# Half-height rotary score matmuls, run as pairs in the two row halves of TensorE

## The chip, the cores and the metric

The kernel runs on one core of a Trainium2 chip. The metric is device time in microseconds (us) of one execution; several executions are timed and their median is taken. Beside them stands one execution recorded by the hardware profiler, with every instruction of the engines: TensorE (PE, with its weight loads as PEld), VectorE (DVE), ScalarE (ACT), GpSimd (POOL) and the queue engine SyncE (SP).

## What is computed

One encoder layer for two sequences of 1024 tokens and width 1024, in float32. A projection feeds two branches, latent attention with four heads and Fourier mixing; both go through one output projection, then a gated feed-forward part. The change concerns the attention scores only:

```
sc = (einsum('bqhd,bkhd->bhqk', q_nope, k_nope)
      + einsum('bqhr,bkr->bhqk', q_pe, k_pe)) * scale
p = softmax(sc, axis=-1)
o = einsum('bhqk,bkhd->bqhd', p, v)
```

The first product goes over 128 latent values per head, the second over the 64 rotary values (ROPE_DIM = 64) of the query `q_pe` and of the key `k_pe`, which all heads share.

## The kernel before

To keep float32 precision with the fast matmul type, each operand is split into a high and a low part, and a product is made of high*high, high*low and low*high (`mm3`, lines 78 to 80; `split`, lines 62 and 63, is an ACT cast followed by a DVE subtraction).

The program runs in stages: input projection and Fourier input, Fourier output, attention with the output projection, then feed-forward for both sequences. The attention stage handles 64 items in the order sequence s (2), query block b (4 of 256 rows), head h (4), query tile u (2 of 128 rows). Item k = 8*(4*s + b) + 2*h + u. I call the eight items of one query block a batch.

For item k the main loop issues, in this order: `scores(k)`; parts of the preparation of the next batch's queries (`rope_q`, `rope_flip`); after an odd item `absorb_q` of the next head (L78 to L80, `gb<-wq,ql`, followed by the split into `qa`); `flip_p(k-1)`, which turns the probabilities of the item before by eight TensorE transposes (L929, `ppt<-ident,p`); after a whole head `values` (L78 to L80, `gb<-pt,ckv`, 24 matmuls); and a step of the output projection and second norm of an older batch (`out_step`: 12 matmuls `gb<-wv,o`, then L813, and per row tile `norm2` with the square sum L821 on ACT, the reciprocal root on POOL L102 to L109 and the scaling L823 `xn` on DVE, then the transposes L833). A scheduler may shift the order inside each engine; each engine then runs its own list strictly in order.

`scores` of an item makes a tile `ps_s` of 128 queries x 1024 keys in PSUM, of which there are two buffers. Each half of 512 keys is summed by five matmuls, L903 to L907: three for the latent part (`qa`), two for the rotary part (`qp`). The rotary operands use all 128 rows of the array: rows 0 to 63 of `qp` hold the high part of q_pe, rows 64 to 127 the low part, and both row halves of `lat[i][:, 1]` hold the same 64 rows of k_pe, in its high part for i = 0 and its low part for i = 1. So L906 gives (high + low)*high, and L907 (high + low)*low. Then the softmax follows: the maximum on DVE (L912 `mx`), its scaled negative (L913 `nb`), the exponential with the row sum on ACT (L915, two records: ACTIVATE and the reading of the accumulator), the reciprocal (L916 `rr`) and the scaling (L917 `p`) on DVE. The exponential is the last reader of the `ps_s` tile; a tile's buffer is free for other scores only behind it.

Of the kernel before, what the change touches and what calls it, by code (L numbers as in the profile page):

```python
# [12 lines left out]
F32 = mybir.dt.float32  # L13
# [3 lines left out]
ALU = mybir.AluOpType  # L17
# [4 lines left out]
P = 128  # L22
D = 1024
N = 1024
# [28 lines left out]
def hybrid_encoder_kernel(ctx: ExitStack, tc: tile.TileContext, a: dict):  # L53
    nc = tc.nc
# [3 lines left out]
    def rd(t):  # L58
        return t.bitcast(F32)
# [17 lines left out]
    def mm3(out, lh, ll, rh, rl, first, last, cont=False):  # L77
        nc.tensor.matmul(out, lh, rh, start=first, stop=False, skip_group_check=cont)  # L78
        nc.tensor.matmul(out, lh, rl, start=False, stop=False, skip_group_check=cont)  # L79
        nc.tensor.matmul(out, ll, rh, start=False, stop=last, skip_group_check=cont)  # L80
# [82 lines left out]
    with ExitStack() as st:  # L163
# [3 lines left out]
        pp = st.enter_context(tc.tile_pool(name="p1_ps", bufs=8, space=PSUM, reuse_waits="tile"))  # L167
# [394 lines left out]
    S = {}  # L562
# [11 lines left out]
    def half(name):  # L574
        return e.tile([P, 512], F32, tag="hv", name=name, bufs=2)
# [34 lines left out]
    with ExitStack() as st:  # L610
# [3 lines left out]
        pp = st.enter_context(tc.tile_pool(name="p2_ps", bufs=8, space=PSUM, reuse_waits="tile"))  # L614
# [179 lines left out]
    def gbank():  # L794
        return tl_ps.tile([P, 512], F32, tag="g", name="gb", bufs=2)
# [55 lines left out]
    with ExitStack() as st:  # L851
        w = st.enter_context(tc.tile_pool(name="p3", bufs=1, side="right", reuse_waits="tile"))
        pp = st.enter_context(tc.tile_pool(name="p3_ps", bufs=1, space=PSUM, reuse_waits="tile"))
        st.enter_context(E3)

        def rope_q(s, b, u):
            ql = S["q", s, b]
            ti = 2 * b + u
            us = slice(u * P, u * P + P)
            pq = gbank()  # L860
            for c in range(2):
                mm3(pq[:, :256], ql[0][:, c, us], ql[1][:, c, us], wq_h[:, c, 512:], wq_l[:, c, 512:], c == 0, c == 1)
            pv = pq[:, :256].rearrange("p (h r) -> p h r", h=HEADS)
            t1 = half("qt1").rearrange("p (k h r) -> p k h r", k=2, h=HEADS)
            cb = rc[:, ti : ti + 1, :].broadcast_to([P, HEADS, ROPE])
            sb = rs[:, ti : ti + 1, :].broadcast_to([P, HEADS, ROPE])
            nc.vector.tensor_tensor(out=t1[:, 0], in0=pv, in1=cb, op=ALU.mult)
            nc.vector.tensor_tensor(out=t1[:, 1, :, :32], in0=pv[:, :, 32:], in1=sb[:, :, :32], op=ALU.mult)
            nc.vector.tensor_tensor(out=t1[:, 1, :, 32:], in0=pv[:, :, :32], in1=sb[:, :, 32:], op=ALU.mult)
            here["p"] = nc.gpsimd.tensor_tensor(out=t1[:, 0], in0=t1[:, 0], in1=t1[:, 1], op=ALU.add).ins  # L870
            sk = w.tile([P, HEADS, P], F32R, tag="sk", name="qsk", bufs=2)
            nc.scalar.copy(sk[:, :, :64], t1[:, 0])
            nc.vector.tensor_tensor(out=sk[:, :, 64:], in0=t1[:, 0], in1=rd(sk[:, :, :64]), op=ALU.subtract)
            S["sk", s, b, u] = sk

        def rope_flip(s, b, u):
# [8 lines left out]
        def absorb_q(s, b, h):  # L885
# [6 lines left out]
            split(qa[0], qa[1], pq[:, :256])  # L892
            S["qa", s, b, h] = qa

        def scores(s, b, h, u):
            lat = S[s][0]
            qa, qp = S["qa", s, b, h], S["qp", s, b, u]
            us = slice(u * P, u * P + P)
            ps = pp.tile([P, N], F32, tag="s", name="ps_s", bufs=2)
            for g in range(2):  # L900
                gs = slice(512 * g, 512 * g + 512)
                o = ps[:, gs]
                nc.tensor.matmul(o, qa[0][:, us], lat[0][:, 0, gs], start=True, stop=False)  # L903
                nc.tensor.matmul(o, qa[0][:, us], lat[1][:, 0, gs], start=False, stop=False)
                nc.tensor.matmul(o, qa[1][:, us], lat[0][:, 0, gs], start=False, stop=False)
                nc.tensor.matmul(o, qp[:, h, :], lat[0][:, 1, gs], start=False, stop=False)  # L906
                nc.tensor.matmul(o, qp[:, h, :], lat[1][:, 1, gs], start=False, stop=True)  # L907
            mx = tiny.tile([P, 1], F32, name="mx")
            nb = tiny.tile([P, 1], F32, name="nb")
            sm = tiny.tile([P, 1], F32, name="sm")  # L910
            rr = tiny.tile([P, 1], F32, name="rr")
            nc.vector.tensor_reduce(out=mx, in_=ps, axis=AX.X, op=ALU.max)  # L912
            nc.vector.tensor_scalar(out=nb, in0=mx, scalar1=-SCALE, scalar2=None, op0=ALU.mult)  # L913
            p = w.tile([P, N], F32, tag="p", name="p", bufs=3)
            nc.scalar.activation(p, ps, AF.Exp, bias=nb, scale=SCALE, accum_out=sm)  # L915
            nc.vector.reciprocal(rr, sm)  # L916
            nc.vector.tensor_scalar(out=p, in0=p, scalar1=rr[:, 0:1], scalar2=None, op0=ALU.mult)  # L917
            S["p", s, b, h, u] = p
            S["rr"] = rr
# [23 lines left out]
        for u in range(2):  # L943
            rope_q(0, 0, u)
# [52 lines left out]
        for k in range(nit + 4):  # L997
# [7 lines left out]
            if k < nit:  # L1005
                s, b, h, u = items[k]
                scores(s, b, h, u)
                nxt = items[k + 8 - k % 8] if k + 8 - k % 8 < nit else None
                i = k % 8
                if nxt is not None:  # L1010
                    if i == 0:
                        load_q(*nxt[:2])
                    if i == 3 and nxt[1] == 0:
                        load_seq(nxt[0], w)
                    if i in (3, 4):
                        rope_q(*nxt[:2], i - 3)
                    if i in (5, 6):
                        rope_flip(*nxt[:2], i - 5)
                if u == 1 and k + 1 < nit:
                    absorb_q(*items[k + 1][:3])  # L1020
# [14 lines left out]
    with ExitStack() as st:  # L1035
# [139 lines left out]
        pp = st.enter_context(tc.tile_pool(name="p5_ps", bufs=8, space=PSUM, reuse_waits="tile"))  # L1175
# [455 lines left out]
```

## Time and profile before

| what | value |
|---|---|
| median of the 3 timed runs | 2117.27 us (2114.76 to 2119.18) |
| span of the profiled execution, first to last instruction | 2109.8 us |
| PE busy in it | 2033.0 us (96%), 10044 matmuls |
| DVE / ACT / POOL busy | 67% / 43% / 39% |
| attention stage, first to last score matmul | about 335 to 764 us |
| PE busy in 335 to 764 us | 412.72 of 429 us |
| mean granted TensorE clock of the core | 0.988 |

The page gives no other time for the profiled execution than its span; the timed runs lie some 7.5 us above it, which is what lies around the first and the last instruction. A matmul record lasts longer than its slot, since matmuls overlap in the array: a record of 128x512 lasts 0.39 us, but the next one starts 0.23 us later. So what a matmul costs is read from the distance of the starts.

### The profile page before, as it was taken

The page shows a single profiled execution, that of the slowest core. Times are in us where ns is not written, and L with a number is a line of the kernel's source. Part 1 is how long each engine was busy: PE and PEld are TensorE (multiplying, and loading weights), DVE is VectorE, ACT ScalarE, POOL GpSimd, SP SyncE. Part 2 cuts the span into 40 slices and gives each one's busy share as a digit, 9 for nine tenths or more (in the row PEclk, how much of TensorE's full clock was granted, in tenths as well). Part 3 has the DMA queues.
Part 4 walks back from the last instruction along what each step waited for, and adds up shares of the span by engine and source line. Part 5 has one row for each costly group of instructions (what it writes and reads, how often), then busy time and mean ns, then how long its engine had stood idle before and what let it go on. Part 6 is the DMA issues. An engine that isn't in the chain of part 4 may idle for free. (4 is left out here: it accounts for less than half of the span.)

```text
span 2109.8 us, 28784 instructions
## 1 busy us (share of the span) xinstructions
PE 2033.0 (96%) x10044; PEld 1667.0 (79%) x10044; DVE 1414.4 (67%) x2087; ACT 906.0 (43%) x1763; POOL 828.6 (39%) x1018
## 2 busy tenths in 40 slices
PE   5899998999999999999999999999999999999998
PEld 2788876888888887788888888887788888888886
DVE  2657756766676678777677677777766666566685
ACT  2656534555565555232333346453233333336441
POOL 1455202111311314888778610235544454420142
PEclk8999999999999999999999999999999999999999
DMA  9575765544544455554554578674332232247772
GB/s 368 194 248 190 248 233 197 113 88 91 159 119 118 150 186 211 180 193 169 194 185 166 174 250 270 222 236 164 131 119 90 91 125 95 81 154 280 233 227 99
DMA packets 184254, 371.30 MB, mean 176 GB/s; under 512 B 19052, under 2 KB 58604, under 8 KB 181036
## 3 DMA queue, kind: packets, MB, share of 16 engines
q1 hardware_dynamic: 166252, 314.00, 44.1%
q0 software_dynamic: 17856, 55.45, 8.9%
q8 instruction: 79, 1.29, 0.2%
q14 instruction: 67, 0.55, 0.1%
HBM read 257.38 MB, written 120.39 MB: 179 GB/s over the span
## 5 line engine op out<-in xcount | busy, mean ns | idle before, releaser
L78 PE MATMUL bank<-H,wh 128*128 128x512 f32 x1232 | 489.6, 398 | 7.7 <-ACT val L1311 4.0
L80 PE MATMUL bank<-H,wl 128*128 128x512 f32 x1232 | 488.9, 397 | 1.4 <-DVE wl L63 1.4
L79 PE MATMUL bank<-H,wh 128*128 128x512 f32 x1232 | 489.0, 397 | 0.0
L137 DVE TENSOR_TENSOR val<-bank,val 128x512 f32<-128x512 f32 x244 | 167.1, 690 | 185.7 <-PE bank L80 178.6
L78 PEld LDWEIGHTS bank<-H,wh 128*128 128x128 f32 x1232 | 232.5, 189 | 66.8 <-ACT val L1311 5.4
L80 PEld LDWEIGHTS bank<-H,wl 128*128 128x128 f32 x1232 | 232.5, 189 | 57.9 <-DVE wl L63 1.7
L79 PEld LDWEIGHTS bank<-H,wh 128*128 128x128 f32 x1232 | 232.7, 189 | 56.2
L63 DVE TENSOR_TENSOR wl<-draw,wh 128x512 fp32r<-128x512 f32 x286 | 203.1, 744 | 82.7 <-ACT wh L62 80.7
L62 ACT CAST wh<-draw 128x512 fp32r<-128x512 f32 x286 | 168.8, 619 | 159.0 <-PE bank L79 83.0
L137 POOL TENSOR_TENSOR val<-val 128x512 f32<-128x512 f32 x58 | 82.9, 1438 | 366.3 <-DVE val L1412 187.6
L79 PE MATMUL bank<-wl,wh 128*128 128x512 f32 x572 | 223.8, 391 | 1.6 <-DVE wl L63 1.6
L80 PE MATMUL bank<-wh,wl 128*128 128x512 f32 x572 | 222.7, 389 | 0.0
L78 PE MATMUL bank<-wh 128*128 128x512 f32 x572 | 222.6, 389 | 0.0
L62 ACT CAST wh<-rgu 128x512 fp32r<-128x512 f32 x172 | 106.7, 621 | 269.7 <-PE bank L79 209.5
L62 ACT CAST wh<-val 128x512 fp32r<-128x512 f32 x133 | 82.2, 622 | 280.5 <-PE bank L79 249.1
L63 DVE TENSOR_TENSOR wl<-val,wh 128x512 fp32r<-128x512 f32 x133 | 141.5, 1066 | 85.6 <-ACT wh L62 85.5
L63 DVE TENSOR_TENSOR wl<-rgu,wh 128x512 fp32r<-128x512 f32 x172 | 169.4, 985 | 4.9 <-ACT wh L62 4.8
L134 POOL TENSOR_TENSOR val<-rgu 128x512 f32<-128x512 f32 x84 | 122.8, 1462 | 125.0 <-DMA rgu<-in_wgu_dram 108.8
L79 PEld LDWEIGHTS bank<-wl,wh 128*128 128x128 f32 x572 | 107.4, 188 | 27.3 <-DVE wl L63 5.3
L78 PEld LDWEIGHTS bank<-wh 128*128 128x128 f32 x572 | 107.4, 188 | 22.4
L80 PEld LDWEIGHTS bank<-wh,wl 128*128 128x128 f32 x572 | 107.4, 188 | 22.0
L134 POOL TENSOR_TENSOR val<-val 128x512 f32<-128x512 f32 x89 | 119.4, 1357 | 1.3
(332 smaller groups left out, 4051.2 us busy)
## 6 DMA issues: line engine op xcount, KB each, us to landing
rgu<-in_wgu_dram SPq DMA_DIRECT2D x86, 512.0 KB
draw<-s_d SPq DMA_DIRECT2D x143, 256.0 KB
s_d<-val POOLq DMA_DIRECT2D x88, 256.0 KB, 4.1
draw<-t_d SPq DMA_DIRECT2D x88, 256.0 KB
s_d<-val SPq DMA_DIRECT2D x66, 256.0 KB
draw<-in_w_down_dram SPq DMA_DIRECT2D x55, 256.0 KB
wada<-in_w_ada_dram SPq DMA_DIRECT2D x13, 1024.0 KB
xt<-in_x_dram SPq DMA_DIRECT2D x16, 512.0 KB
```

Source lines behind the costliest of these rows:

```text
L62: here["a"] = nc.scalar.copy(hi, src).ins
L63: here["v"] = nc.vector.tensor_tensor(out=lo, in0=src, in1=rd(hi), op=ALU.subtract).ins
L78: nc.tensor.matmul(out, lh, rh, start=first, stop=False, skip_group_check=cont)
L79: nc.tensor.matmul(out, lh, rl, start=False, stop=False, skip_group_check=cont)
L80: nc.tensor.matmul(out, ll, rh, start=False, stop=last, skip_group_check=cont)
L134: return eng.tensor_tensor(out=out, in0=x, in1=y, op=ALU.subtract).ins
L137: eng.tensor_tensor(out=out, in0=x, in1=y, op=ALU.add)
```

## The change

The product low*low of the rotary part is left out: the second rotary pass is now high*low alone, over 64 rows. For the query tile u = 0 the high part lies in rows 0 to 63 as before; for u = 1 it is written into rows 64 to 127 (the index `k ^ u` in `rope_q`). `scores` with u = 0 now also issues the second rotary pass of both tiles: for each half of the keys one matmul on rows 0 to 63 into the tile's own bank, and one on rows 64 to 127 that opens the sum in the bank of the tile u = 1. `scores` with u = 1 then adds its eight other matmuls to that bank.

```diff
--- before.py
+++ after.py
@@ -869,8 +869,9 @@
             nc.vector.tensor_tensor(out=t1[:, 1, :, 32:], in0=pv[:, :, :32], in1=sb[:, :, 32:], op=ALU.mult)
             here["p"] = nc.gpsimd.tensor_tensor(out=t1[:, 0], in0=t1[:, 0], in1=t1[:, 1], op=ALU.add).ins
             sk = w.tile([P, HEADS, P], F32R, tag="sk", name="qsk", bufs=2)
-            nc.scalar.copy(sk[:, :, :64], t1[:, 0])
-            nc.vector.tensor_tensor(out=sk[:, :, 64:], in0=t1[:, 0], in1=rd(sk[:, :, :64]), op=ALU.subtract)
+            hi, lo = (sk[:, :, 64 * (k ^ u) : 64 * (k ^ u) + 64] for k in range(2))
+            nc.scalar.copy(hi, t1[:, 0])
+            nc.vector.tensor_tensor(out=lo, in0=t1[:, 0], in1=rd(hi), op=ALU.subtract)
             S["sk", s, b, u] = sk
 
         def rope_flip(s, b, u):
@@ -892,19 +893,28 @@
             split(qa[0], qa[1], pq[:, :256])
             S["qa", s, b, h] = qa
 
+        def score_bank():
+            return pp.tile([P, N], F32, tag="s", name="ps_s", bufs=2)
+
         def scores(s, b, h, u):
             lat = S[s][0]
             qa, qp = S["qa", s, b, h], S["qp", s, b, u]
             us = slice(u * P, u * P + P)
-            ps = pp.tile([P, N], F32, tag="s", name="ps_s", bufs=2)
+            ps = score_bank() if u == 0 else S.pop("ps")
             for g in range(2):
                 gs = slice(512 * g, 512 * g + 512)
                 o = ps[:, gs]
-                nc.tensor.matmul(o, qa[0][:, us], lat[0][:, 0, gs], start=True, stop=False)
+                nc.tensor.matmul(o, qa[0][:, us], lat[0][:, 0, gs], start=u == 0, stop=False)
                 nc.tensor.matmul(o, qa[0][:, us], lat[1][:, 0, gs], start=False, stop=False)
                 nc.tensor.matmul(o, qa[1][:, us], lat[0][:, 0, gs], start=False, stop=False)
-                nc.tensor.matmul(o, qp[:, h, :], lat[0][:, 1, gs], start=False, stop=False)
-                nc.tensor.matmul(o, qp[:, h, :], lat[1][:, 1, gs], start=False, stop=True)
+                nc.tensor.matmul(o, qp[:, h, :], lat[0][:, 1, gs], start=False, stop=u == 1)
+            if u == 0:
+                pn, qn = score_bank(), S["qp", s, b, 1]
+                for g in range(2):
+                    gs = slice(512 * g, 512 * g + 512)
+                    nc.tensor.matmul(ps[:, gs], qp[:64, h, :], lat[1][:64, 1, gs], start=False, stop=True)
+                    nc.tensor.matmul(pn[:, gs], qn[64:, h, :], lat[1][64:, 1, gs], start=True, stop=False)
+                S["ps"] = pn
             mx = tiny.tile([P, 1], F32, name="mx")
             nb = tiny.tile([P, 1], F32, name="nb")
             sm = tiny.tile([P, 1], F32, name="sm")
```

In the changed file the five lines of the score matmuls are L907 to L910 and, for the pair, L915 (rows 0 to 63) and L916 (rows 64 to 127); the transposes of the probabilities are L939, the softmax steps L922 (`mx`), L923 (`nb`), L925 (exponential), L926 and L927. There are 33 runs of the half-height matmuls in PE's list: 31 times L915, L916, L915, L916 without anything between, and one head in which they stand apart. From the end of the attention stage on, PE's order is the same in both programs.

The first place is on PE, at the second half of the keys of an even item (k = 18). Before, five score matmuls, four matmuls of `values`, then the transposes of the probabilities of item 17:

```order
L903 MATMUL ps_s<-lat_3403,qa_4876 128x512
L904 MATMUL ps_s<-lat_3404,qa_4876 128x512
L905 MATMUL ps_s<-lat_3403,qa_4877 128x512
L906 MATMUL ps_s<-lat_3403,qp 128x512
L907 MATMUL ps_s<-lat_3404,qp 128x512
L78 MATMUL gb<-pt_4744,ckv_3405 128x256
L79 MATMUL gb<-pt_4745,ckv_3405 128x256
L80 MATMUL gb<-pt_4744,ckv_3406 128x256
L78 MATMUL gb<-pt_4744,ckv_3405 128x256
L929 MATMUL ppt<-ident,p 128x128 x8
```

The same place in the changed program:

```order
L907 MATMUL ps_s<-lat_3403,qa_4876 128x512
L908 MATMUL ps_s<-lat_3404,qa_4876 128x512
L909 MATMUL ps_s<-lat_3403,qa_4877 128x512
L910 MATMUL ps_s<-lat_3403,qp 128x512
L915 MATMUL ps_s<-lat_3404,qp 128x512
L916 MATMUL ps_s<-lat_3404,qp 128x512
L915 MATMUL ps_s<-lat_3404,qp 128x512
L916 MATMUL ps_s<-lat_3404,qp 128x512
L939 MATMUL ppt<-ident,p 128x128 x8
L78 MATMUL gb<-pt_4744,ckv_3405 128x256
L79 MATMUL gb<-pt_4745,ckv_3405 128x256
```

The four half-height matmuls stand behind the eight full ones, and the four matmuls of `values` that stood ahead of the transposes now stand behind them.

The second place is on DVE, at the last item of a batch (k = 23): `x` is the output projection's row tile, `xn` its scaling, `mx` and `nb` the softmax steps of item 23, `qa` the low part of the next head's query. Before:

```order
L813 TENSOR_TENSOR x_5029<-x_5029,gb 128x512
L823 TENSOR_SCALAR xn<-x_5029,rs_r 128x1024
L912 TENSOR_REDUCE mx<-ps_s 128x1
L63 TENSOR_TENSOR qa_5374<-gb,qa_5373 128x256
L913 TENSOR_SCALAR nb<-mx 128x1
L63 TENSOR_TENSOR pt_5378<-ppt,pt_5377 128x4x128 x2
```

In the changed program:

```order
L813 TENSOR_TENSOR x_5029<-x_5029,gb 128x512
L922 TENSOR_REDUCE mx<-ps_s 128x1
L823 TENSOR_SCALAR xn<-x_5029,rs_r 128x1024
L923 TENSOR_SCALAR nb<-mx 128x1
L63 TENSOR_TENSOR qa_5374<-gb,qa_5373 128x256
L63 TENSOR_TENSOR pt_5378<-ppt,pt_5377 128x4x128
```

The maximum has moved ahead of `xn`. The same swap is there at items 15, 31, 47 and 55; at item 39 the maximum stood ahead of `xn` before already.

The third place is on PE in the first batch, at the item k = 4. Before, its last score matmuls:

```order
L905 MATMUL ps_s<-lat_3403,qa_3860 128x512
L906 MATMUL ps_s<-lat_3403,qp 128x512
L907 MATMUL ps_s<-lat_3404,qp 128x512
L903 MATMUL ps_s<-lat_3403,qa_3859 128x512
L904 MATMUL ps_s<-lat_3404,qa_3859 128x512
L905 MATMUL ps_s<-lat_3403,qa_3860 128x512
L906 MATMUL ps_s<-lat_3403,qp 128x512
L907 MATMUL ps_s<-lat_3404,qp 128x512
```

In the changed program:

```order
L909 MATMUL ps_s<-lat_3403,qa_3860 128x512
L910 MATMUL ps_s<-lat_3403,qp 128x512
L915 MATMUL ps_s<-lat_3404,qp 128x512 x2
L78 MATMUL gb<-pt_3754,ckv_3405 128x256
L939 MATMUL ppt<-ident,p 128x128 x8
L79 MATMUL gb<-pt_3755,ckv_3405 128x256
L80 MATMUL gb<-pt_3754,ckv_3406 128x256
L78 MATMUL gb<-pt_3754,ckv_3405 128x256
L916 MATMUL ps_s<-lat_3404,qp 128x512 x2
```

Here the two matmuls on rows 0 to 63 and the two on rows 64 to 127 are not neighbours.

## The prediction

> **What bounds the kernel now.** I read the page first, then the windows over the attention stage, then its waits on PE, and last the timeline at single places.
>
> ```profile
> PE 2033.0 (96%) x10044; PEld 1667.0 (79%) x10044; DVE 1414.4 (67%) x2087; ACT 906.0 (43%) x1763; POOL 828.6 (39%) x1018
> ```
>
> ```profile
> 335.00:764.00 429.00, 412.72 (x2574) 363.22 (x2575) 293.65 (x548) 233.24 (x479) 96.61 (x154) 0.99 0.46 122
> ```
>
> ```profile
> PE ps_s L905 <- DVE nb L913: 7.4, 5, 2.1
> ...
> PE ppt L929 <- DVE p L917: 2.1, 8, 0.6
> ```
>
> PE is busy for 96% of the span, and for 412.72 of 429 us in the stage that changes (the second fence: length, then busy time of PE, PEld, DVE, ACT, POOL). So a PE slot saved there is time saved, unless PE then waits for the softmax. The two waits say where the softmax is close: five times L905, the first reader of a query's low part, waits for a DVE that is behind with an old maximum (7.4 us as recorded), and eight times the transposes wait for scaled probabilities (2.1 us). Only this stage matters, since PE's list is the same behind it.
>
> **The slots removed.** The starts of neighbouring score matmuls:
>
> ```profile
> 560.11 0.39 PE L906 MATMUL ps_s<-lat,qp 128*128 128x512 f32 x1
> 560.34 0.40 PE L907 MATMUL ps_s<-lat,qp 128*128 128x512 f32 x1
> 560.58 0.28 PE L78 MATMUL gb<-ql,wq_h 128*128 128x256 f32 x1
> ```
>
> A slot is 0.23 us. Each of the 32 heads has four L907, 0.93 us; in their place come four half-height matmuls. If the two of a pair run side by side, they fill two slots, 0.46 us, so the change removes 32 x 0.46 = 14.7 us of slots at most.
>
> **The price of the half-height group.** No matmul of before uses half of the rows. The nearest are those of few columns: L760 and L309 work on four quarters and two halves of the columns, each between full matmuls.
>
> ```profile
> 268.18 0.40 PE L80 MATMUL bank<-wm,B 128*128 128x512 f32 x1
> 268.51 0.16 PEld L760 LDWEIGHTS bank<-wada,scT 128*32 128x32 f32 x8 [0.36 <-issue]
> 268.51 1.92 PE L760 MATMUL bank<-wada,scT 128*32 128x512 f32 x16
> 268.96 0.13 PEld L760 LDWEIGHTS bank<-wada,scT 128*32 128x32 f32 x4 [0.30 <-issue]
> 269.39 0.13 PEld L760 LDWEIGHTS bank<-wada,scT 128*32 128x32 f32 x4 [0.30 <-issue]
> 270.36 0.50 PE L78 MATMUL bank<-wm,A 128*128 128x512 f32 x1
> 270.70 0.39 PE L79 MATMUL bank<-wm,A 128*128 128x512 f32 x1
> ```
>
> The weight loads show a beat of 0.43 us with four loads each. Sixteen matmuls one after the other would take 16 x 0.43 = 6.9 us; they take 1.92, about four beats, so four tiles do run side by side. The switch is not free: from the start of L80 (268.18) to that of the second full matmul behind (270.70) are 2.52 us; less two full slots (0.46) and four beats (1.72) there remain 0.34. The second case:
>
> ```profile
> 162.98 1.04 PE L380 MATMUL bank<-ident,xt 128*128 128x128 f32 x8
> 163.94 1.94 PE L309 MATMUL bank<-wada,lw 128*64 128x512 f32 x8
> 165.81 0.40 PE L78 MATMUL bank<-wcs_h,eoh 128*128 128x280 f32 x1
> 166.05 0.29 PE L79 MATMUL bank<-wcs_l,eoh 128*128 128x280 f32 x1
> ```
>
> Eight transposes of about 0.11 end their slots at 163.86; to 166.05 are 2.19 us, less one slot of 280 columns (0.13) and four beats (1.72): again 0.34. So going into a divided array and back costs about 0.34 us, with uncovered weight loads of 32 or 64 columns. Here the loads have 128 columns; a transpose slot, which holds a 128-column load, is 0.11 us, so I add 0.1. The group then takes 0.46 + 0.34 + 0.1 = **0.90 us** against 0.93. The bounds: 0.46 if nothing is paid; 0.93 + 0.34 = 1.27 if the halves run in turn; and 2.3 if each of the three further changes of half inside a group costs 0.34 too. I take 0.90, since both rows show overlap and a price. The Trainium skill bears on this: its page "TensorEngine Tiling (Array Packing)", section "Key Properties", says that a change of the tiling mode, though not of the tile, drains TensorE. By that rule the group pays once on each side, which the two rows agree with, and the sum is the one below.
>
> **Where a head can't be faster: the softmax of the odd item.** The new bank of tile u = 1 is opened already inside u = 0, one item early, and it is the buffer of the odd item before; so the first L916 waits for that item's exponential, with all of PE's list queued behind it. The place where least work lies between is after an odd item with only `absorb_q` and the transposes (eleven heads by PE's order: items 6, 8, 10, 18, 26, 34, 42, 50, 58, 60 and 62). Item 33 and then 34:
>
> ```profile
> 560.77 1.23 DVE L912 TENSOR_REDUCE mx<-ps_s 128x1 f32<-128x1024 f32 x1 [1.84 <-PE ps_s L907]
> 562.09 0.49 PE L903 MATMUL ps_s<-lat,qa 128*128 128x512 f32 x1
> 562.89 1.14 ACT L915 ACTIVATE p<-ps_s,nb 128x1024 f32<-128x1024 f32 x1
> 563.90 0.21 ACT L915 ACTIVATION_READ_ACCUMULATOR p<-ps_s,nb 128x1 f32 x1
> 564.04 0.40 PE L906 MATMUL ps_s<-lat,qp 128*128 128x512 f32 x1
> 564.35 0.88 DVE L917 TENSOR_SCALAR p<-p,rr 128x1024 f32<-128x1024 f32 x1
> 564.50 0.28 PE L78 MATMUL gb<-pt,ckv 128*128 128x256 f32 x1
> 564.62 0.28 PE L79 MATMUL gb<-pt,ckv 128*128 128x256 f32 x1
> 565.37 1.06 PE L929 MATMUL ppt<-ident,p 128*128 128x128 f32 x8 [0.24 <-DVE p L917]
> ```
>
> Item 33 ends at 560.34, its exponential at 564.11. In the changed program the scores of item 34 start at 562.09 again, and behind eight matmuls the group begins where the ninth stands now, at 564.04. Its L916 can go at about 564.15, a delay of at most 0.1, and the group ends at 564.95 to 565.05. The transposes behind it need `p` (ready 565.23) and start at 565.37, as before. The four `values` matmuls that now fill this wait (0.12 each, 564.50 to 564.62) stand behind the transposes instead: +0.47; the next item has two matmuls less: -0.46. **Eleven heads: 0.** The cover is gone here: any group up to about 1.2 us gives the same time, a longer one is paid in full.
>
> **A stall that goes.** The last item of a batch, item 23:
>
> ```profile
> 488.92 0.48 PE L903 MATMUL ps_s<-lat,qa 128*128 128x512 f32 x1
> 491.10 0.39 PE L907 MATMUL ps_s<-lat,qp 128*128 128x512 f32 x1
> 492.47 0.19 POOL L109 TENSOR_TENSOR rs_r<-rs_w,rs_y 128x1 f32<-128x1 f32 x1
> 492.56 0.41 ACT L62 CAST qa<-gb 128x256 fp32r<-128x256 f32 x1
> 492.70 0.75 DVE L823 TENSOR_SCALAR xn<-x,rs_r 128x1024 f32<-128x1024 f32 x1 [3.68 <-ACT ht L836]
> 493.37 1.22 DVE L912 TENSOR_REDUCE mx<-ps_s 128x1 f32<-128x1024 f32 x1
> 493.49 0.40 PE L904 MATMUL ps_s<-lat,qa 128*128 128x512 f32 x1
> 494.50 0.41 DVE L63 TENSOR_TENSOR qa<-gb,qa 128x256 fp32r<-128x256 f32 x1
> 494.97 0.50 PE L905 MATMUL ps_s<-lat,qa 128*128 128x512 f32 x1 [1.08 <-DVE nb L913]
> 497.41 1.04 PE L929 MATMUL ppt<-ident,p 128*128 128x128 f32 x8
> ```
>
> DVE stands idle for 3.68 us in front of `xn`, whose factor comes from POOL at 492.66; the maximum, whose scores are ready at 491.5 (0.43 behind the last score matmul, as from 560.34 to 560.77), is queued behind it, then `qa`, and PE's L905 waits for that. In the changed program the maximum is ahead of `xn`. It starts at about 491.1 (the item has two matmuls less and ends near 490.6) and is done at 492.3, in the idle time; `xn` runs 492.70 to 493.45 as now, `nb` ends at 493.5, `qa` at 493.9, and L905's successor starts at 494.0 instead of 494.97. Behind it come six matmuls (1.4) and the group (0.9): the transposes start at 496.3, against 497.41. The bank is free then: the exponential can start at 493.6 and ends its reading near 494.8, ahead of the group at 495.4. Gain 1.1 us. Its bounds are 0 (DVE late with something else) and 1.25, the time that L905 starts behind its place (493.49 + 0.23). The swap is at five items (15, 23, 31, 47, 55): **-5.3 us**, rounding 1.05 each. At item 39 the order was so already: 0.
>
> **The rest.** Twelve heads with the output projection ahead of them have the bank long free: 12 x (0.90 - 0.93) = **-0.4**. In the head of item 4 the matmuls of the two halves stand apart: two trips into the divided array and no pair, 0.93 + 2 x 0.34 - 0.93 = **+0.7**. The first two heads: 0 (bounds -1 and +2; DVE's list is reordered there). The cast and the subtraction in `rope_q` keep their sizes: 0. No DMA is added or moved. The sum is -5.3 - 0.4 + 0.7 = **-5.0 us**. The span would go from 2109.8 to 2104.8; with the 7.5 us around it, the median from 2117.27 to **2112.3**.
>
> **The rivals.**
> - *No price for the switch.* The group takes 0.46. Beside the 5.3 of the stalls come 12 x 0.47 = 5.6, at the six ends of batches 6 x 0.44 = 2.6, nothing at the eleven, and 0.5 at the start, where the 0.7 is not paid: -14.0, **2103.3**. Against it stand the 0.34 of both rows; for it, that those divide the columns and this the rows. The Trainium skill's page "TensorE: Matmul & The Clock Gate", section "Measured speedup vs the span model", counts a pack as one matmul and about 4 ns per further tile, with no such price; by that rule this rival holds, and on the two column cases the trace does not agree. Chance 0.16.
> - *The stall stays.* DVE is late with something else, the 5.3 are lost: **2117.6**. For it: L905 waited in one such place at item 39 too. Chance 0.17.
> - *The halves run in turn, one price per group* (the change then doesn't do what it says): 1.27 each, 0.37 more at 12 + 6 + 2 heads (+7.4) and 0.1 at the eleven (+1.1): -5.0 + 8.5 = +3.5, **2120.8**. Chance 0.09.
> - *The slower side: each change of half drains the array.* The place is between L915 and L916, the price up to 0.34 three times per group. At 0.15 each, with the halves in turn, a group is 1.7: 12 x 0.8 + 6 x 0.8 + 11 x 0.5 + 2 for the start = 22 more than the forecast: +17, **2134**. It decides from about 1.33 per group: 18 x 0.43 + 11 x 0.13 = 9.2, which lifts -5.0 to +4.2. Against it: four column tiles in a row show no drain between them. Chance 0.18.
>
> **How the numbers follow.** A measurement of this kernel can tell about 0.2% (4.2 us) from no change: below 2113.0 is faster, above 2121.5 slower. The forecast has 0.40; its own spread (2108 to 2116, mainly the gain per stall and the 0.1 of the loads) lies for 0.25 below 2113.0. Faster: 0.25 + 0.16 = 0.41. Slower: 0.18 + 0.03 of the third rival's upper part = 0.21. Same: the remaining 0.38. The range, 2103 to 2126, takes in all but the larger part of the last rival.
>
> **What would show it.** In the changed profile: L916 starts within 0.12 us of its L915, and the next full matmul about 0.9 us behind the group's start (step 2; 0.46, 1.27 or 1.7 give the rivals). The wait of L909 for DVE shrinks from 7.4 to some 2 us, `mx` standing ahead of `xn` in the idle time. The first L916 shows waits for ACT of at most 0.2 us, and the transposes behind still wait at the eleven heads. Waits of L916 of 0.5 us or more would prove the third step wrong.

## The result and the profile after

The changed kernel takes 2112.66 us (median of 20 runs, 2107.09 to 2115.78), the kernel before beside it 2115.38 us (20 runs, 2113.93 to 2119.18): a ratio of 0.9985, with a 95% interval of 0.9978 to 0.9992, 0.15% less. The span of its profiled execution is 2110.1 us, against 2109.8 before. So little happened in sum. Behind it stand a gain of 7.0 us and a loss of 3.7 to 7.7 us, and the prediction saw the gain only.

The page's first line and the window over the attention stage, of the changed kernel:

```profile
PE 2030.9 (96%) x10044; PEld 1650.1 (78%) x10044; DVE 1412.7 (67%) x2087; ACT 905.3 (43%) x1763; POOL 827.4 (39%) x1018
```

```profile
335.00:764.00 429.00, 412.59 (x2597) 348.62 (x2596) 298.81 (x553) 234.63 (x483) 96.05 (x154) 0.99 0.47 126
```

The count of matmuls is the same, 10044, and PE is as busy in this window as before (412.72). Its waits in the same window, with the total, the count and the longest of each:

```profile
PE gb L78 <- DVE qt L869: 4.9, 1, 4.9
PE ppt L939 <- DVE p L927: 4.2, 12, 0.4
PE ppt L939 <- DVE pt L63: 2.8, 1, 2.8
PE ps_s L907 <- ACT qa L62: 2.4, 2, 2.0
PE ps_s L909 <- DVE qa L63: 2.4, 3, 1.0
```

The wait for a late maximum (7.4 us, five times) is gone; L909 keeps 2.4 us. The transposes now wait twelve times for `p`, 4.2 us against 2.1. This view lists no wait of L916 for a bank, but the timeline has a short one (below). The first row was there before (5.4 us). New is the third, one wait of 2.8 us, and the fourth has grown from 0.7 us (both are of the start of the stage; the longest wait in the fourth is 2.0).

The timeline of item 23, up to the group of item 24, shows the steps that were forecast: start, duration, engine, line.

```profile
491.12 0.48 PE L907 MATMUL ps_s<-lat,qa 128*128 128x512 f32 x1
...
493.26 1.23 DVE L922 TENSOR_REDUCE mx<-ps_s 128x1 f32<-128x1024 f32 x1 [2.05 <-PE ps_s L910]
...
494.67 0.19 POOL L109 TENSOR_TENSOR rs_r<-rs_w,rs_y 128x1 f32<-128x1 f32 x1
...
494.89 0.75 DVE L823 TENSOR_SCALAR xn<-x,rs_r 128x1024 f32<-128x1024 f32 x1 [0.41 <-POOL rs_r L109]
...
496.10 0.50 PE L909 MATMUL ps_s<-lat,qa 128*128 128x512 f32 x1
...
497.36 0.40 PE L910 MATMUL ps_s<-lat,qp 128*128 128x512 f32 x1
497.69 0.18 PEld L915 LDWEIGHTS ps_s<-lat,qp 64*128 64x128 f32 x1 [0.36 <-issue]
497.69 0.50 PE L915 MATMUL ps_s<-lat,qp 64*128 64x512 f32 x1
497.69 0.18 PEld L916 LDWEIGHTS ps_s<-lat,qp 64*128 64x128 f32 x1
497.69 0.73 PE L916 MATMUL ps_s<-lat,qp 64*128 64x512 f32 x2
...
498.03 0.39 PE L915 MATMUL ps_s<-lat,qp 64*128 64x512 f32 x1
498.35 0.86 PEld L939 LDWEIGHTS ppt<-ident,p 128*128 128x128 f32 x8 [0.36 <-issue]
498.35 1.09 PE L939 MATMUL ppt<-ident,p 128*128 128x128 f32 x8
```

The maximum runs in the idle time ahead of `xn`, and from the first score matmul of the item (491.12) to the transposes of the next (498.35) are 7.23 us; before it was 8.49 (488.92 to 497.41). L915 and L916 start together, weight loads included. The second pair follows after 0.34, the transposes after another 0.32, and the first pair came 0.33 behind L910, where a full slot is 0.23.

In the eleven heads that the prediction named as tight the first L916 starts 0.03 to 0.10 us behind its L915, and some 0.05 behind the end of the exponential that frees its bank (its second record, the reading of the accumulator). Item 34:

```profile
563.09 0.21 ACT L925 ACTIVATION_READ_ACCUMULATOR p<-ps_s,nb 128x1 f32 x1
563.32 0.50 PE L915 MATMUL ps_s<-lat,qp 64*128 64x512 f32 x1
563.35 0.49 PE L916 MATMUL ps_s<-lat,qp 64*128 64x512 f32 x1
```

In the other heads whose four matmuls stand together the two start within 0.01 us of each other.

To see where the time went I cut the span at three starts in PE's timeline, the first score matmul of items 0, 8 and 63. Before:

```profile
335.00 0.50 PE L903 MATMUL ps_s<-lat,qa 128*128 128x512 f32 x1 [0.37 <-ACT qa L62]
...
381.04 0.48 PE L903 MATMUL ps_s<-lat,qa 128*128 128x512 f32 x1
...
761.53 0.39 PE L903 MATMUL ps_s<-lat,qa 128*128 128x512 f32 x1
```

After:

```profile
334.67 0.51 PE L907 MATMUL ps_s<-lat,qa 128*128 128x512 f32 x1 [0.38 <-ACT qa L62]
...
384.40 0.48 PE L907 MATMUL ps_s<-lat,qa 128*128 128x512 f32 x1
...
757.93 0.39 PE L907 MATMUL ps_s<-lat,qa 128*128 128x512 f32 x1
```

From item 0 to 8 the change costs 3.7 us (46.04 to 49.73), from 8 to 63 it gains 7.0 (380.49 to 373.53). What lies behind item 63 is 1348.3 before (2109.8 - 761.53) and 1352.2 after, and this part is scatter: over all profiles of this study it lies between 1346.9 and 1352.8, in no order that follows the kernels (the kernel before has 1351.4 in its second profile). That is why the profiled span is no shorter. So below the experiments are read from the two first parts, from one profile each, and the medians stand beside them.

| kernel | median, us | ratio, 95% interval | item 0 to 8 | item 8 to 63 |
|---|---|---|---|---|
| before; its second profile | 2115.38 | | 46.04; 44.79 | 380.49; 380.57 |
| changed; its second profile | 2112.66; 2113.47 | 0.9985 (0.9978 to 0.9992) | 49.73; 52.47 | 373.53; 373.69 |
| before, maximum ahead | 2105.55 | 0.9955 (0.9943 to 0.9968) | 45.51 | 372.60 |
| changed, maximum behind as before | 2121.63 | 1.0029 (1.0018 to 1.0040) | 50.84 | 380.57 |
| changed, no pairs | 2120.17 | 1.0026 (1.0015 to 1.0037) | 50.31 | 381.58 |
| changed, other order of the four | 2107.82 | 0.9968 (0.9957 to 0.9980) | 45.98 | 373.55 |
| changed, GpSimd's weights held back | 2111.77 | 0.9978 (0.9969 to 0.9987) | 48.36 | 374.24 |
| changed, all weights held back | 2101.55 | 0.9935 (0.9923 to 0.9947) | 40.62 | 374.06 |
| before, maximum ahead and weights held back | 2100.93 | 0.9940 (0.9927 to 0.9952) | 43.19 | 373.28 |
| the same with the values ahead | 2099.99 | 0.9936 (0.9923 to 0.9948) | 42.95 | 370.93 |
| changed, weights held back, values ahead | 2096.78 | 0.9923 (0.9910 to 0.9937) | 40.15 | 370.37 |

Each ratio is to runs of the kernel before beside it (medians 2113.27 to 2115.96), so medians of different rows compare to 1 or 2 us only.

### The profile page after: what moved, and what is told of

The parts are those of the page before. It is cut to its first block, busy times and chain, and to the rows that moved or that the text cites. A ratio compares the mean times of both kernels' runs of the same rounds, so it can differ in the third digit from the quotient of the medians.

```text
span 2110.1 us, 28795 instructions
## 1 busy us (share of the span) xinstructions
PE 2030.9 (96%) x10044; PEld 1650.1 (78%) x10044; DVE 1412.7 (67%) x2087; ACT 905.3 (43%) x1763; POOL 827.4 (39%) x1018
## 5 line engine op out<-in xcount | busy, mean ns | idle before, releaser
L63 DVE TENSOR_TENSOR wl<-val,wh 128x512 fp32r<-128x512 f32 x133 | 131.7, 992 | 83.0 <-ACT wh L62 83.0
L63 DVE TENSOR_TENSOR wl<-rgu,wh 128x512 fp32r<-128x512 f32 x172 | 174.9, 1017 | 5.5 <-ACT wh L62 5.5
```

Of the source, the lines that this page charges most:

```text
L63: here["v"] = nc.vector.tensor_tensor(out=lo, in0=src, in1=rd(hi), op=ALU.subtract).ins
```

## The experiments

My theory after the result: the gain is the maximum's place ahead of `xn`; the pairs overlap but pay almost all of it back; and work on the output weights, which moved ahead of attention work at the start of the stage, eats most of the gain. The rivals: the pairs carry the gain themselves, or the start is noise.

In the diffs below, `first(x, y)` is a helper of the program that makes the scheduler list `x` ahead of `y` on their engine, without a wait.

**1. Both kernels once more.** No edit.

> The changed kernel once more, for a second profile and a closer time. Stall theory (the gain comes from the five stalls of 1.2 us at the last item of a batch, the pairs are worth what they replace, and the start of the attention stage loses 4 us): 3.7 us less than before in the attention stage, first score matmul at about 335 us, item 63 at 758 to 759; whole kernel 0.10 to 0.20% faster. If the feed-forward stage is really longer behind the change (1350.5 against 1346.2 us in the first two profiles), it is 4 us longer here too; if that was the scatter of one execution, it lies anywhere between 1343 and 1352.

> The kernel before once more, for a second profile. If the work behind the attention stage scatters by itself, it takes 1347 to 1352 us here as in the other profiles (1347.1 in the first profile of before, 1349.5 to 1351.9 in five others); if the changed order in the attention stage lengthens it, it is again near 1347.

The changed kernel: 2113.47 us (ratio 0.9993, 0.9982 to 1.0004). Its second profile has 373.69 us from item 8 to 63, 0.16 off the first, and before's 0.08 off; so that part repeats to some 0.2 us. The start repeats worse (49.73 and 52.47; 46.04 and 44.79), but the two kernels stay apart by 3.7 us at least. The second interval takes in 1, so the gain in sum is hardly clear of the noise; the two parts are.

**2. The maximum ahead, without pairs.** The kernel before, and at items 15, 23, 31, 47 and 55:

```diff
-            nc.vector.tensor_reduce(out=mx, in_=ps, axis=AX.X, op=ALU.max)
+            red = nc.vector.tensor_reduce(out=mx, in_=ps, axis=AX.X, op=ALU.max).ins
+            if (s, b, h, u) in [(0, 1, 3, 1), (0, 2, 3, 1), (0, 3, 3, 1), (1, 1, 3, 1), (1, 2, 3, 1)]:
+                first(red, here["n"][1])
```

> The kernel before, with the softmax maximum put ahead of the scaling of the normed rows on DVE at the five items 15, 23, 31, 47, 55; no half-height matmuls. Stall theory: each of these five ends of a batch takes about 1 us less (12.4 us for the two items to about 11.4), in all 4 to 6 us, so 0.2 to 0.3% faster than before. Rival, the pairs bring the gain: no change within 0.05%.

2105.55 us. From item 8 to 63 it takes 372.60, 7.9 us less than before, and 0.9 less than the changed kernel. That is more than the 4 to 6 us expected. One line of order gives more than the whole change.

**3. The pairs, without the maximum ahead.** The changed kernel, with the old order at the five items:

```diff
-            nc.vector.tensor_reduce(out=mx, in_=ps, axis=AX.X, op=ALU.max)
+            red = nc.vector.tensor_reduce(out=mx, in_=ps, axis=AX.X, op=ALU.max).ins
+            if (s, b, h, u) in [(0, 1, 3, 1), (0, 2, 3, 1), (0, 3, 3, 1), (1, 1, 3, 1), (1, 2, 3, 1)]:
+                first(here["n"][1], red)
```

> The changed kernel with the old order on DVE at the same five items, the scaling of the normed rows ahead of the maximum. Stall theory: the stalls return, 5 x 1.2 = 6 us slower than the changed kernel, so 2 to 3 us slower than before (+0.10 to +0.15%). Rival, the pairs bring the gain: no slower than the changed kernel, 0.10 to 0.15% faster than before.

2121.63 us, slower than before. Its waits of PE from item 8 on, up to 760 us:

```profile
PE ps_s L909 <- DVE nb L925: 7.4, 5, 2.1
PE ppt L941 <- DVE p L929: 5.6, 11, 1.1
```

The old 7.4 us are back, five times, and item 8 to 63 takes 380.57, to 0.1 us what the kernel before takes. So behind the start the pairs are worth nothing in sum in this order, and the gain there is the maximum's place. What is lost in total is the start: 50.84 against 46.04 and 44.79, 4.8 to 6.1 us; so the median lies 5.7 us above the runs of the kernel before (2115.96), not 2 to 3 as expected.

**4. No pairs: both tiles in rows 0 to 63.** The same four half-height matmuls, now one after the other:

```diff
-            hi, lo = (sk[:, :, 64 * (k ^ u) : 64 * (k ^ u) + 64] for k in range(2))
+            hi, lo = (sk[:, :, 64 * k : 64 * k + 64] for k in range(2))
...
-                    nc.tensor.matmul(pn[:, gs], qn[64:, h, :], lat[1][64:, 1, gs], start=True, stop=False)
+                    nc.tensor.matmul(pn[:, gs], qn[:64, h, :], lat[1][:64, 1, gs], start=True, stop=False)
```

> The changed kernel with both query tiles' high part in rows 0 to 63: the same matmuls of half height in the same order, but all in one row half, so that no two can run side by side. Pair theory of the group (the two halves run together, the switch costs about 0.34 us once a group): the group takes about 0.4 us more (some 1.3 instead of 0.87), paid at the 12 heads with output projection and the 6 ends of batches, little at the eleven tight heads: 8 to 10 us slower than the changed kernel, +0.25 to +0.35% against before. Rival, the halves ran in turn already: the time of the changed kernel within 0.1%.

2120.17 us, and 381.58 from item 8 to 63, 8.1 more than with pairs. The timeline of PE at the group ahead of the transposes of an item:

```profile
502.11 0.40 PE L910 MATMUL ps_s<-lat,qp 128*128 128x512 f32 x1
502.43 0.49 PE L915 MATMUL ps_s<-lat,qp 64*128 64x512 f32 x1
502.77 0.39 PE L916 MATMUL ps_s<-lat,qp 64*128 64x512 f32 x1
503.00 0.39 PE L915 MATMUL ps_s<-lat,qp 64*128 64x512 f32 x1
503.23 0.39 PE L916 MATMUL ps_s<-lat,qp 64*128 64x512 f32 x1
503.56 1.09 PE L939 MATMUL ppt<-ident,p 128*128 128x128 f32 x8
```

From L910 to the transposes are 1.45 us, with pairs 0.99 (497.36 to 498.35). The difference, 0.46, is two slots: the halves do run side by side. The distances also show the price: 0.32 into the group and 0.34 to its second matmul, where a slot is 0.23, then 0.23 and 0.23, and 0.33 out of it. It is paid on the way in and out, 0.1 us each time, whatever the rows of the neighbours inside are, so a change of the half within the group costs nothing. This agrees with the Trainium skill in its page "TensorEngine Tiling (Array Packing)", section "Key Properties", by which a change of the mode drains and a change of the tile doesn't: the first has a price here, the second none. The page gives no price.

The head steps tell where such slots count. With pairs taken away, the steps around nine of the eleven tight heads change by 0.05 us at most (for example items 17 to 19: 10.33 to 10.38); items 6 and 34 grow by 0.39 and 0.46. The loose ones grow by 0.41 to 0.56 (items 11 to 13: 16.90 to 17.46).

**5. Another order of the four.** First the two matmuls of rows 0 to 63, then the two of rows 64 to 127:

```diff
                     nc.tensor.matmul(ps[:, gs], qp[:64, h, :], lat[1][:64, 1, gs], start=False, stop=True)
+                for g in range(2):
+                    gs = slice(512 * g, 512 * g + 512)
                     nc.tensor.matmul(pn[:, gs], qn[64:, h, :], lat[1][64:, 1, gs], start=True, stop=False)
```

> The changed kernel with the four half-height matmuls in the order first half, first half, second half, second half of the rows. If only neighbours in PE's order can run together, two slots stay alone and one pair forms in the middle: three slots instead of two, 0.23 us more a group, 4 to 5 us slower than the changed kernel. If each half of the array has a queue of its own and all four can be in flight, no change. If each change of half cost a drain, this order with one change instead of three would be faster than the changed kernel.

2107.82 us, about 5 less than the changed kernel, and yet 373.55 from item 8 to 63, the same to 0.02. So of the three cases expected it is the one without a change: all four can be in flight. A group of this run, in whose list both L915 stand ahead of both L918 (rows 64 to 127):

```profile
408.00 0.49 PE L915 MATMUL ps_s<-lat,qp 64*128 64x512 f32 x1
408.01 0.50 PE L918 MATMUL ps_s<-lat,qp 64*128 64x512 f32 x1
408.34 0.39 PE L915 MATMUL ps_s<-lat,qp 64*128 64x512 f32 x1
408.35 0.40 PE L918 MATMUL ps_s<-lat,qp 64*128 64x512 f32 x1
```

The first L918 starts 0.33 us ahead of the second L915, which stands before it in the list. So PE does not start the matmuls of different row halves strictly in the order of its list.

The difference lies in the start, 45.98. There the scheduler happened to list GpSimd's work as in the kernel before. GpSimd's rows, the kernel before first (`qt` is the rotary add of the queries, `wvr` the multiplication of output weights):

```profile
347.30 0.73 POOL L870 TENSOR_TENSOR qt<-qt 128x256 f32<-128x256 f32 x1 [0.94 <-DVE qt L869]
349.94 5.90 POOL L973 TENSOR_TENSOR wvr<-wvr,gah 128x512 f32<-128x512 f32 x4 [1.92 <-DMA gah<-ga_d]
```

The changed kernel:

```profile
348.99 6.16 POOL L983 TENSOR_TENSOR wvr<-wvr,gah 128x512 f32<-128x512 f32 x4 [3.53 <-DMA gah<-ga_d]
355.12 0.72 POOL L870 TENSOR_TENSOR qt<-qt 128x256 f32<-128x256 f32 x1
```

This run:

```profile
347.27 0.73 POOL L870 TENSOR_TENSOR qt<-qt 128x256 f32<-128x256 f32 x1 [0.94 <-DVE qt L869]
349.92 5.92 POOL L985 TENSOR_TENSOR wvr<-wvr,gah 128x512 f32<-128x512 f32 x4 [1.92 <-DMA gah<-ga_d]
```

In the changed kernel `qt` stands behind four multiplications that wait for a DMA, and comes 7.8 us later. ACT's list is as before too: three casts of output weights ahead of the stage's first exponential, where the changed kernel has four. This run is the change without its accident: 6.9 us gained behind the start, nothing lost in it, 2107.82 beside 2114.34 us of the kernel before.

**6. GpSimd's weights held back.** The second multiplication is put behind `qt`, its load one step of the list later:

```diff
-                nc.gpsimd.tensor_tensor(out=raw, in0=raw, in1=S["ga"], op=ALU.mult)
+                mul = nc.gpsimd.tensor_tensor(out=raw, in0=raw, in1=S["ga"], op=ALU.mult).ins
+                if (s, g) == (0, 1):
+                    first(here["p"], mul)
...
-            todo[2 * g].append(lambda g=g: gate_half(0, g))
-            todo[2 * g].append(lambda g=g: wv_load(0, g))
+            todo[3 * g].append(lambda g=g: gate_half(0, g))
+            todo[3 * g].append(lambda g=g: wv_load(0, g))
```

> The changed kernel with the second group of four output-weight multiplications on POOL put behind the rotary addition of the next batch's first query tile, as in the kernel before. POOL-queue theory of the lost start (the rotary addition stands 6 us behind those multiplications, and ACT, the transposes' buffers and PE behind it): item 3 starts 3 to 4 us earlier than in the changed kernel, the whole is 0.15 to 0.2% faster than the changed kernel, so 0.3 to 0.35% faster than before. Rival, the start is lost by the half-height matmuls that stand apart at item 4, or by DVE's order of the weight splits: less than 1 us gained.

2111.77 us; the start takes 48.36, between the two kernels. It gained less than expected, 0.22% against the kernel before and not 0.3 to 0.35. In the profiles this edit gets back 1.4 to 4.1 us (from 49.73 and 52.47), and the start of the changed kernel alone scatters by 2.7. `qt` comes as early as in the kernel before (346.97 us) and PE's wait for `pt` falls from 2.8 to 0.9 us, but the one of 2.0 for `qa` stays: four casts of weights still stood ahead of ACT's first exponential. So GpSimd's list is only a part of the loss.

**7. All weights held back.** Beside the edit of 6, the splits of these weights on ACT and DVE are listed behind the attention's current work (`behind` is a helper of the program):

```diff
-        def wv_split(i):
+        def wv_split(i, hold=False):
...
-            split(wv[0][:, h, gs], wv[1][:, h, gs], S.pop(("wv", h, g)))
+            with behind() if hold else ExitStack():
+                split(wv[0][:, h, gs], wv[1][:, h, gs], S.pop(("wv", h, g)))
...
-            todo[3 + i].append(lambda i=i: wv_split(i))
+            todo[3 + i].append(lambda i=i: wv_split(i, True))
```

> The run after_start with the output-weight splits of the first sequence also kept behind the probability splits issued ahead of them on ACT and DVE. Weight-split theory of the lost start (the splits and multiplications of the output weights had moved ahead of attention work in three lists): the start is regained, item 8 starts no more than 46.5 us behind item 0 (before 46.0, changed 49.7 and 52.5), and the whole is 0.3 to 0.45% faster than before. Rival, the start is lost by the pairs themselves, which take the odd item's bank early: item 8 stays at 48 us or later.

2101.55 us, and 40.62 us for the start, 4.2 to 5.4 less than before the change, and more than expected. The windows tell why it is more than the waits. Length, busy PE, PEld, DVE, ACT, POOL, then the granted clock of TensorE and the DMA's share and GB/s. The kernel before:

```profile
345.00:350.00 5.00, 2.36 (x8) 1.91 (x9) 4.27 (x12) 4.97 (x10) 2.14 (x3) 0.50 0.32 104
350.00:355.00 5.00, 5.00 (x20) 4.24 (x19) 4.71 (x6) 3.25 (x6) 5.00 (x4) 0.58 0.01 2
355.00:365.00 10.00, 9.75 (x65) 8.64 (x64) 8.99 (x18) 6.08 (x11) 0.84 (x1) 1.00 0.37 133
```

The second profile of the changed kernel:

```profile
345.00:350.00 5.00, 1.62 (x6) 1.35 (x6) 3.20 (x9) 4.01 (x6) 1.35 (x2) 0.50 0.33 105
350.00:355.00 5.00, 4.49 (x15) 3.58 (x16) 3.24 (x4) 1.35 (x5) 5.00 (x4) 0.56 0.60 211
355.00:365.00 10.00, 7.28 (x29) 5.74 (x28) 6.52 (x11) 5.27 (x10) 1.30 (x2) 0.66 0.08 26
```

All weights held back:

```profile
345.00:350.00 5.00, 3.47 (x19) 2.05 (x18) 2.71 (x5) 1.65 (x4) 2.84 (x3) 1.00 0.19 72
350.00:355.00 5.00, 4.64 (x25) 3.71 (x25) 5.00 (x10) 2.89 (x5) 4.21 (x4) 1.00 0.09 34
355.00:365.00 10.00, 10.00 (x74) 8.77 (x73) 9.11 (x19) 6.83 (x14) 2.02 (x2) 1.00 0.12 28
```

PE waits for `qt` in the kernel before too (5.4 us here, 5.2 in this profile of the changed kernel), and in both its clock is at half for ten us, from about 344 to 354; in the changed kernel's second profile it is at half once more, for 7 us from 358 on (0.66). With the weights held back no wait there is longer than 1.1 us, the clock stays at 1.00, and PE does 118 matmuls in these 20 us, against 93 and 50.

**8. The best arrangement, with and without pairs.** First the kernel before with the edits of 2 and 7:

> The kernel before, without any pair, with the two side effects alone: the maximum ahead of the block's normalised copy at the five last items, and the output-weight work of the first sequence held back behind the attention's. It is the changed kernel with the weights held back (2101.55 us; 40.62 us from the first scores to item 8, 374.06 us from item 8 to item 63), less the pairs. Theory (the pairs themselves are worth nothing in the span, since what a group saves at a loose head, 0.1 us, is given back in waits behind the pairs at a tight one): 41 us to item 8, 372.6 us from item 8 to item 63 as in the run with the maximum ahead alone, a time of 2100 to 2102 us. Rival (the pairs carry a gain of their own): 374 to 380 us from item 8 to item 63 and a time of 2103 to 2108 us.

2100.93 us, and 373.28 from item 8 to 63, where the changed kernel with weights held back has 374.06 and 2101.55. Without pairs it is as fast as with them.

Then, to fill the waits for `p`, both with the 24 `values` matmuls ahead of the transposes at ten tight items (k is the item, `values` and the transposes stand in this loop):

```diff
+            ahead = k in (8, 10, 18, 26, 34, 42, 50, 58, 60, 62)
+            if ahead:
+                values(*items[k - 3][:3])
...
-            if 0 <= k - 3 < nit and (k - 3) % 2 == 1:
+            if 0 <= k - 3 < nit and (k - 3) % 2 == 1 and not ahead:
```

> The same kernel without pairs, and at ten tight items the 24 value matmuls of the item before stand ahead of the eight transposes. The run with the maximum ahead alone shows only 1.0 us of waits of the transposes for the softmax's p (six of 0.2 us), since four value matmuls stand in that gap already. Theory (the tight heads are bound by the softmax only through this gap): 0 to -1 us from item 8 to item 63, so 371.6 to 372.6 us and a time about 0.5 us under that of the kernel without this edit. Rival (transposes that come late hold up the copies and the values behind them): 373 to 377 us.

> The changed kernel, pairs and all, with the output-weight work held back (2101.55 us) and the 24 value matmuls ahead of the eight transposes at the same ten items. Its trace without this edit shows 4.8 us of waits of the transposes for p, twelve of them, 0.3 to 0.9 us each. Theory (what the pairs save at the tight heads is lost in this gap, and comes out when the gap is filled): 3 to 4 us less from item 8 to item 63, so 370 to 371 us where the kernel without this edit has 374.06, and a time of 2097.5 to 2099; with pairs then 1 to 2 us ahead of the same arrangement without them, 32 groups at 0.87 us in place of 0.93. Rival (a change of the tile's height costs more than the group shows, for instance in the transposes behind it): 373 to 374 us and 2101 us, no better than without pairs.

Without pairs 2099.99 us and 370.93 from item 8 to 63; with pairs 2096.78 and 370.37, the fastest of all. PE's waits from item 8 on, in the latter:

```profile
PE ps_s L909 <- DVE qa L63: 2.4, 3, 1.0
PE ppt L939 <- DVE p L927: 0.7, 2, 0.3
```

The twelve waits for `p` are down to two, and 3.7 us are gained with pairs (374.06 - 370.37), as expected. Without pairs it is 2.4 (373.28 - 370.93), more than the 0 to 1 expected; ahead of this edit that kernel waited longer for `p` than the 1.0 us of run 2:

```profile
PE ppt L931 <- DVE p L919: 1.9, 7, 0.9
```

The pairs are in the end worth 0.6 us in this part (370.93 - 370.37), less than the 1 to 2 expected. The medians differ by 3.2, of which 2.8 lie in the start (42.95 and 40.15). There the two lists differ and the start scatters by as much; no run shows whether any of it is the pairs' own.

## Why the prediction came out as it did

The time was forecast to 0.4 us (2112.3, measured 2112.66), and that is luck. The forecast took 5.0 us off the first three runs of the kernel before, 2117.27; the 20 runs beside the changed kernel have 2115.38, so the gain is 2.7 us. And this gain comes of two errors of opposite sign: the gain in the middle is larger than forecast, and the start loses what it took for nothing.

- **What bounds the stage, slot of 0.23 us:** borne out. Two slots more per group (experiment 4) cost 0.41 to 0.56 us at a loose head.
- **Price of the group, 0.90 against 0.93:** right, for about the reason given. From L910 to the matmul behind the group are 0.98 to 0.99 us in the 16 heads behind the start where nothing waits, and less L910's own slot 0.75. A further 0.10 shows between the next two matmuls where these have 256 columns (0.22 apart, 0.12 before), and 0.06 where they are transposes. That is 0.81 to 0.86: two slots and a price of 0.35 to 0.40, a little less than the 0.44 forecast. The group starts L915 and L916 together, as the sign named for it said. The other sign, 0.9 us from the group's start to the next full matmul, was badly put: that distance is 0.66 (497.69 to 498.35), since a part of the price lies ahead of the group and a part behind the matmul that follows it. The price that the two column cases showed held for the row halves, and "no price" (0.46) failed. So did the Trainium skill's page "TensorE: Matmul & The Clock Gate", section "Measured speedup vs the span model", as a price of a mixed program: where no bank is waited for, the tiles of a pair do start within 0.01 us of each other, as its 4 ns per tile say, but the way in and out, which it doesn't count, takes back 0.35 to 0.40 of the 0.46.
- **Eleven tight heads, 0:** right. Items 17 to 19: 10.36 before, 10.33 after; 25 to 27: 10.34 and 10.34. Eight of the eleven changed by 0.05 at most; item 6 gained 0.3, and items 34 and 58 scatter by 0.1 to 0.4 between two profiles of the kernel before. The delay of the first L916 by its bank, at most 0.1 in the forecast, is 0.03 to 0.10 in just these eleven heads. The cover was as said: 0.46 more per group changed nine of them by nothing, and the wait for `p` takes up the difference (4.2 us with pairs; 0.3 us in experiment 4).
- **Five stalls, -1.05 each:** the mechanism right, the size a little low. Items 15 to 17 went from 12.41 to 11.19, 23 to 25 from 12.38 to 11.17, 31 to 33 from 12.39 to 11.19, 47 to 49 from 13.89 to 12.64 and 55 to 57 from 13.89 to 12.62: -6.2 in all against -5.3. Experiments 2 and 3 show that this is the maximum's place alone. Without pairs it gives 1.3 to 1.6 each. The pairs take 0.1 to 0.3 of that back: at items 47 and 55 the transposes start at the same time behind the first scores, 8.6 us, since `p` sets it, but three `values` matmuls (0.35) that stood ahead of them in the run without pairs now stand behind. At item 39, forecast at 0, 0.24 is lost (11.38 to 11.62).
- **Loose heads, -0.4 in all:** right in kind; 0.03 to 0.13 us each against run 2 (items 11 to 13: 17.03 there, 16.90 after), 0.8 us for the twelve.
- **The parted head of item 4, +0.7:** right. Items 4 to 6: 11.31 before, 11.97 after.
- **The first two heads, 0 with bounds of -1 and +2: this step failed.** The start lost 3.7 to 7.7 us, of which 0.7 are item 4's. I had seen that DVE's list is reordered there, and priced only that. Not read was GpSimd's list, in which `qt` fell behind four multiplications of weights, nor ACT's, where a fourth cast of weights slipped ahead of the first exponential. PE then waits 2.0 us for `qa`, at half the clock, and 2.8 for `pt`; in the second profile the clock is at half once more behind that. Run 5 shows that it is an accident of the list and no price of the pairs.
- **DMA and what follows the stage, 0:** nothing in the two speaks against it, but single spans differ there by up to 5.9 us for an unchanged order of PE, so no term of an us or two could be seen.

The forecast for the part from item 8 to 63 was -5.3 - 0.4 = -5.7, measured -7.0; for the part ahead of it +0.7, measured +3.7 (49.73 - 46.04) to +7.7 (52.47 - 44.79). What stays open: why the scheduler turned the three lists at the start when two matmuls moved (run 5 shows how little is needed), and which of the lists on ACT and DVE costs how much; runs 6 and 7 take GpSimd apart from the others only.

## What to carry to other kernels

Ask of a half-array pair what the way in and out costs before counting the slots: two pairs between full matmuls save 0.46 us and pay 0.35 to 0.40. By these numbers a longer run of divided matmuls would gain more for the same price; no run here has tried one. When a change shifts a scheduler's lists, read every engine's list where the pipeline starts up, since weight preparation that slipped ahead of attention work cost about as much there as the change gained in 55 items. And look whether a side effect is the gain: one maximum listed ahead of a waiting scaling, at five places, gave more than the pairs that brought it about.

## What the runs showed of the hardware

Matmuls on the two row halves start at the same time, with their weight loads (497.69 for all four records), and a change of the half costs nothing, while a change between 128 and 64 rows costs about 0.1 us at the group's first matmul, at its second and at the first full one behind, and 0.06 to 0.10 at the one after that. Between the halves the order of the list does not hold: in run 5 the first matmul on rows 64 to 127 started 0.33 us ahead of one on rows 0 to 63 that stands before it.

I had not expected how much a single wait costs PE at this place: behind 5.2 us without work (the changed kernel's second profile) the granted clock was 0.50 in one stretch of 5 us and 0.56 in the next. The Trainium skill's page "TensorE: Matmul & The Clock Gate", section "What's actually happening", states such a halving after an idle window of about 3.4 us. The traces agree in the halving, and its stretches here last 3.4, 6.8 or 10.2 us; but the length of the wait alone does not decide it. PE's wait for `pt`, 2.8 and 2.7 us in the changed kernel's two profiles, left the clock at 1.00 in the first; in the second the clock fell to half during it, for 6.8 us. Removing the long wait (run 7) kept it at 1.00.
